# Five key and query projections as seven-block products, with three kinds of sums on GpSimd and PSUM banks 5+1+1+1

## The chip, the cores and the metric

The kernel runs on one core of a Trainium2 chip. The metric is the device time of one execution in microseconds (us). Engines are named as in the profile: PE is TensorE's matrix multiply and PEld its weight load, DVE is VectorE, ACT is ScalarE, POOL is GpSimd, and SP is SyncE, which here only issues transfers.

## The reference, cut to what matters

The reference is a two-layer encoder over 512 tokens of width 1024. Layer 0 has grouped-query and latent attention, layer 1 has neighbourhood attention (16 heads of 64), and each layer ends in a squared-ReLU MLP. The change touches layer 1's attention alone:

```python
def neighbourhood_attention(h, w_qkv, rpb, w_out):
    q, k, v = jnp.split(h @ w_qkv, 3, axis=-1)      # h is 512 x 1024, w_qkv 1024 x 3072
    ...                                              # 16 heads; 128-query blocks
    sc = jnp.einsum('bhqd,bhqkd->bhqk', qblk, kg) * scale + bias[None]
    p = jax.nn.softmax(sc, axis=-1)
    return jnp.einsum('bhqk,bhqkd->bhqd', p, vg)     # then @ w_out
```

## The kernel before

Every operand of a large product is split into a high and a low part in float32r, and a product is three passes on PE (high by high, high by low, low by high). Activations lie transposed, 1024 features as eight 128-row blocks (KD = 8), 512 tokens along the free axis.

**The seven-block product.** The MLPs of both layers already use class `Seven`. A pair of 128-row blocks of the contraction, a pair of output blocks and two halves of 256 tokens make a 2x2x2 block product, done with seven products of 128x128 by 256 in place of eight. It needs sums of the weight blocks (`seven_chunk`: three POOL operations on 128, 256 and 128 columns, then an ACT copy to the high part and a DVE subtraction to the low part, each on 896 columns), sums of the token blocks (`Seven.sums` and `Seven.split`), and a combination of the seven results (in `Seven.run`).

**Layer 1's attention.** After layer 0's MLP the kernel splits the eight token blocks (`split_g`, into `X`, read as `XP`), and runs two opening products by hand: `valuesC(0)`, the values of heads 0 to 3, and `projC(0)`, the keys and queries of the first pair of heads. While they run, `rows_r1` makes the RMS factor: POOL and DVE sum squares, PE adds them over partitions, DVE turns them into `r1` with three Newton steps (`rsqrt_steps`), and PE transposes `r1` so that `rb` is the factor broadcast over partitions. The order on each engine up to here comes from the tile scheduler.

Then `attend_C` runs the 16 heads one after another with an order fixed by hand (`fixed_order`): every engine does its instructions in the order in which the code emits them. For each head PE computes scores in two halves (`scores`, one `s` bank each), DVE adds the bias and takes the minimum, ACT takes the exponential (`weigh`), DVE the reciprocal, POOL multiplies (`norm`), and one head later PE transposes the result (`turn` with T1 and T2, one `t` bank each) and multiplies with the values (`finish`, one `o` bank). Between these steps `fill.run` places pieces of other products on PE: the seven remaining key and query projections `projC(1)` to `projC(7)`, the values `valuesC(1)` to `valuesC(3)`, and part of the output projection. How much is placed is set by `LEAD` before the first head and by `RATE_C` at six places in every head. Evacuations of these products are put off by `soon` and `soon_a` to the next `catch_up`.

`projC(t)` is a plain product: 8 blocks of the contraction, 2 output blocks (key and query), 3 passes, which is 48 matmuls of 128x512. Its weights come in two chunks of 1024 columns (`chunk`). Its key is evacuated by a DVE multiplication with `rb` and its query by two DVE operations with `rb`, then each is split and sent to the other partitions by transfers from POOL and SP.

PSUM has eight banks: three `mm`, two `s`, two `t` and one `o`, for the whole kernel.

## Time and profile before

| | |
|---|---|
| median of 3 runs | 1154.99 us (1154.98 to 1155.4) |
| span of the profiled execution | 1153.1 us |
| busy PE, DVE, ACT, POOL | 1143.5, 897.7, 668.3, 598.1 us |
| layer 1's 16 heads: first scores to last value product | 618.5 to 794.4 us |
| granted TensorE clock | 0.999 |

The profile has no time of its own for the profiled execution beside its span, which runs from the first to the last instruction; the median of the runs is 1.9 us longer. A duration in the timeline is that of one instruction; matmuls are pipelined, so that their pace is read from the starts of successive ones, not from their durations.

### The profile page before, as it was taken

Reading aid. Unit: us, or ns where it says so; the run is one execution under the profiler, and the core shown is the slowest. Engines: PE = TensorE matmul, PEld = TensorE weight load, DVE = VectorE, ACT = ScalarE, POOL = GpSimd, SP = SyncE. Lnnn points to the kernel's source line nnn. Section 1 sums busy time; section 2 is a strip of 40 time slices with the busy share of each in tenths; the row PEclk is TensorE's granted clock in tenths of the full one; section 3 lists DMA queues with packets and bytes.
Section 4 is the critical chain, followed back from the end, with each engine's and each line's share of the span. In section 5 each row is a group of like instructions: output and inputs, shape, how many; then the busy total and the mean of one; then the engine's idle time right before and its main releaser. Section 6 shows DMA issues by size and latency. Waiting matters only on the chain.

```text
span 1153.1 us, 20506 instructions
## 1 busy us (share of the span) xinstructions
PE 1143.5 (99%) x7348; PEld 1023.9 (89%) x7348; DVE 897.7 (78%) x1570; ACT 668.3 (58%) x1133; POOL 598.1 (52%) x722
## 2 busy tenths in 40 slices
PE   9999999999999999999999999999999999999997
PEld 8787888888899999899988998988889999989996
DVE  7887998988868787978775667668997777697874
ACT  6676786755346668534464556555553666773334
POOL 4356432327688992379432232231388889435740
PEclk9999999999999999999999999999999999999999
DMA  8322441223523335933585564443344233372432
GB/s 237 108 70 76 113 121 56 65 65 99 167 82 93 92 92 151 264 102 99 151 167 158 150 174 128 117 112 116 108 148 128 75 93 91 78 189 70 123 119 73
DMA packets 118325, 136.06 MB, mean 118 GB/s; under 512 B 9923, under 2 KB 99952, under 8 KB 118224
## 3 DMA queue, kind: packets, MB, share of 16 engines
q1 hardware_dynamic: 110736, 119.83, 35.2%
q0 software_dynamic: 7312, 14.83, 6.9%
q8 instruction: 58, 0.95, 0.3%
q14 instruction: 43, 0.35, 0.1%
q10 hardware_dynamic: 176, 0.10, 0.0%
HBM read 112.70 MB, written 6.29 MB: 103 GB/s over the span
## 4 chain that ended last, share of the span: by engine, by line
PE 93%; issue 3%; DVE 2%; ACT 1%; POOL 0%; POOLq 0%; DVEq 0%; ACTq 0%
PE mm L613 9%; PE mm L615 9%; PE mm L614 9%; PE mm L457 4%; PE mm L459 4%; PE mm L458 4%; PE t L457 3%; PE t L459 3%; PE t L458 3%; PE s L1138 3%; PE o L1126 3%; PE s L613 2%; PE s L615 2%; PE s L614 2%; PE s L457 2%
## 5 line engine op out<-in xcount | busy, mean ns | idle before, releaser
L370 DVE TENSOR_TENSOR wlo<-a,whi 128x896 fp32r<-128x896 f32 x106 | 131.4, 1243 | 57.9 <-ACT whi L369 57.5
L613 PE MATMUL mm<-a,whi 128*128 128x512 f32 x428 | 174.1, 407 | 0.1
L614 PE MATMUL mm<-a,whi 128*128 128x512 f32 x428 | 168.8, 394 | 0.0
L615 PE MATMUL mm<-a,wlo 128*128 128x512 f32 x428 | 168.5, 395 | 0.0
L369 ACT ACTIVATE whi<-a 128x896 fp32r<-128x896 f32 x106 | 100.6, 949 | 112.1 <-PE s L458 25.0
L223 DVE TENSOR_TENSOR wlo<-raw,whi 128x1024 fp32r<-128x1024 f32 (+4 forms) x93 | 105.9, 1144 | 27.3 <-ACT whi L233 26.9
L233 ACT ACTIVATE whi<-raw 128x1024 fp32r<-128x1024 f32 (+3 forms) x96 | 88.0, 918 | 59.5 <-PE s L614 24.8
L457 PE MATMUL mm<-a,whi 128*128 128x256 f32 x430 | 120.8, 281 | 0.0
L459 PE MATMUL mm<-a,wlo 128*128 128x256 f32 x430 | 120.6, 280 | 0.0
L458 PE MATMUL mm<-a,whi 128*128 128x256 f32 x430 | 120.5, 280 | 0.0
L369 ACT ACTIVATE whi<-raw 128x896 fp32r<-128x896 f32 x58 | 55.1, 953 | 83.3 <-PE s L458 24.4
L364 POOL TENSOR_TENSOR a<-a 128x256 f32<-128x256 f32 x104 | 95.7, 920 | 8.2
L365 POOL TENSOR_TENSOR a<-a 128x128 f32<-128x128 f32 x104 | 95.5, 919 | 8.2
L615 PEld LDWEIGHTS mm<-a,wlo 128*128 128x128 f32 x428 | 80.3, 188 | 18.3
L613 PEld LDWEIGHTS mm<-a,whi 128*128 128x128 f32 x428 | 80.6, 188 | 16.1 <-issue 0.6
L1146 POOL TENSOR_SCALAR p<-p,ti 128x512 f32<-128x512 f32 x64 | 47.0, 736 | 90.3 <-DVE ti L1145 67.0
L614 PEld LDWEIGHTS mm<-a,whi 128*128 128x128 f32 x428 | 80.7, 189 | 14.6
L370 DVE TENSOR_TENSOR wlo<-raw,whi 128x896 fp32r<-128x896 f32 x58 | 71.5, 1243 | 23.8 <-ACT whi L369 23.7
L1775 POOL TENSOR_SCALAR p<-p,ti 128x256 f32<-128x256 f32 x64 | 35.4, 564 | 104.7 <-DVE ti L1774 91.7
L457 PE MATMUL t<-a,whi 128*128 128x256 f32 x312 | 87.6, 281 | 0.0
L459 PE MATMUL t<-a,wlo 128*128 128x256 f32 x312 | 87.5, 280 | 0.0
L458 PE MATMUL t<-a,whi 128*128 128x256 f32 x312 | 87.5, 280 | 0.0
(449 smaller groups left out, 3602.4 us busy)
## 6 DMA issues: line engine op xcount, KB each, us to landing
a<-in_ffn_w_up_dram SPq DMA_DIRECT2D x102, 256.0 KB, 2.8
raw<-in_ffn_w_down_dram SPq DMA_DIRECT2D x34, 512.0 KB, 4.4
raw<-in_ffn_w_down_dram SPq DMA_DIRECT2D x56, 256.0 KB, 2.7
raw<-in_od_w_qkv_dram SPq DMA_DIRECT2D x64, 128.0 KB, 3.4
raw<-in_ffn_w_up_dram SPq DMA_DIRECT2D x12, 512.0 KB, 4.0
wlo<-in_ffn_w_down_dram POOLq DMA_DIRECT2D x12, 512.0 KB, 6.4
a<-a SPq DMA_DIRECT2D x17, 256.0 KB, 3.3
bx<-a SPq DMA_DIRECT2D x32, 128.0 KB, 5.2
```

What stands on the lines that cost most here:

```text
L223: z = lambda: (eng or DVE).tensor_tensor(to, src, f32(high), op=ALU.subtract)
L233: ACT.activation(hi[:, 0:m], raw[:, 0:m], AF.Copy)
L364: held(eng.tensor_tensor(r[:, 4:6], r[:, 2:3].to_broadcast([P, 2, P]), r[:, 0:7:6], op=ALU.add))
L365: held(eng.tensor_tensor(r[:, 7], r[:, 3], r[:, 5], op=ALU.subtract))
L369: ACT.activation(hi[:, 0:896], raw[:, 128:1024], AF.Copy)
L370: DVE.tensor_tensor(lo[:, 0:896], raw[:, 128:1024], f32(hi[:, 0:896]), op=ALU.subtract)
L457: PE.matmul(o, wh, x[:, 0], start=kp == 0 and n in (0, 1, 3, 5), stop=False, skip_group_check=True)
L458: PE.matmul(o, wh, x[:, 1], start=False, stop=False, skip_group_check=True)
L459: PE.matmul(o, wl, x[:, 0], start=False, stop=kp == self.np - 1, skip_group_check=True)
L613: PE.matmul(o, wh, xh, start=first, stop=False)
L614: PE.matmul(o, wh, xl, start=False, stop=False)
L615: PE.matmul(o, wl, xh, start=False, stop=last)
```

## The change

`projC(1)` to `projC(5)` become `projC7(1)` to `projC7(5)`. Four chunks of weights each (`seven_pair`, three POOL sums per chunk, always in one of four `raw` buffers) and 84 matmuls of 128x256 take the place of two chunks and 48 matmuls of 128x512. The key and query blocks of one pair of heads are the two output blocks of the seven-block product, so it needs four `mm` banks at once. The seven results are combined by four DVE operations, and the multiplications by `rb` move from DVE to POOL. The sums of the token blocks (`SevenC.sums`) are made once, while `projC(0)` runs, with three POOL operations for each of four pairs, and are kept in eight slots until `projC7(5)` has run. For `attend_C` alone the banks become five `mm`, one `s`, one `t` and one `o`. `RATE_C` goes from 1.33 to 1.26, and `valuesC` comes ahead of the projection of the same number.

```diff
+    def banks_for(name, **bufs):
+        psum[0].close()
+        psum[1:] = [psum[0].enter_context(tc.tile_pool(name=name, bufs=1, space=PSUM)), bufs]
+    banks_for("ps", mm=3, s=2, t=2, o=1)
...
+    def seven_pair(w, k0, t):
+        raw = wp.tile([P, 1024], F32, tag="raw", bufs=4, name=nm("raw"))
+        for k in range(2):
...
+        yield
+        POOL.tensor_tensor(r[:, 6], r[:, 0], r[:, 1], op=ALU.subtract)
+        POOL.tensor_tensor(r[:, 4:6], r[:, 2:3].to_broadcast([P, 2, P]), r[:, 0:7:6], op=ALU.add)
+        POOL.tensor_tensor(r[:, 7], r[:, 3], r[:, 5], op=ALU.subtract)
+        yield
...
+        ACT.activation(hi[:, 0:896], raw[:, 128:1024], AF.Copy)
+        yield hi, lo, [lambda: DVE.tensor_tensor(lo[:, 0:896], raw[:, 128:1024], f32(hi[:, 0:896]), op=ALU.subtract)]
...
+    class SevenC(Seven):
...
+        def sums(self, kp):
+            raw, t = Slot(F32), scratch()
+            for z in range(2):
+                ACT.activation(raw.t[:, S * z : S * z + S], hT[:, 2 * kp + z, :], AF.Copy, scale=gmix(1, 2 * kp + z))
+            yield
+            r, t_ = (x.rearrange("p (b n) -> p b n", n=256) for x in (raw.t, t))
+            POOL.tensor_tensor(t_, r[:, 0:1].to_broadcast([P, 2, 256]), r[:, 1:3], op=ALU.subtract)
+            POOL.tensor_tensor(r[:, 0], r[:, 2], t_[:, 0], op=ALU.subtract)
+            POOL.tensor_tensor(r[:, 1], r[:, 3], r[:, 0], op=ALU.subtract)
+            yield
+            for n, src in enumerate((t_, r[:, 0:2])):
...
+                ACT.activation(d[:, :, 0], src, AF.Copy)
+                DVE.tensor_tensor(d[:, :, 1], src, f32(d[:, :, 0]), op=ALU.subtract)
...
+    def projC7(t):
+        ids = [plan(w_qkv, 2 * kp, t, make=seven_pair) for kp in range(4)]
+        def ev(bk, half):
...
+            ACT.activation(Y[:, 0:256], half(bk[0], 0), AF.Copy)
+            def first():
+                DVE.tensor_tensor(two(X), two(Y)[:, 0:1].to_broadcast([P, 2, 256]), two(bk[1]), op=ALU.add)
+                DVE.tensor_tensor(two(Y), two(X)[:, 0:1].to_broadcast([P, 2, 256]), two(bk[2]), op=ALU.add)
+                soon(second)
+            def second():
+                DVE.tensor_tensor(X[:, 0:256], Y[:, 0:256], half(bk[2], 1), op=ALU.add)
+                DVE.tensor_tensor(Y, Y, bk[3], op=ALU.add)
+                POOL.tensor_tensor(nk[:, 0:256], Y[:, 256:512], rb[:, 0:256], op=ALU.mult)
+                POOL.tensor_tensor(nk[:, 256:512], X[:, 256:512], rb[:, 256:512], op=ALU.mult)
+                soon_a(lambda: split(nk, ka, down))
+                POOL.tensor_tensor(nq[:, 64:320], X[:, 0:256], rb[:, 0:256], op=ALU.mult)
+                POOL.tensor_tensor(nq[:, 320:512], Y[:, 0:192], rb[:, 256:448], op=ALU.mult)
+                POOL.tensor_tensor(nq[:, 0:64], Y[:, 192:256], rb[:, 448:512], op=ALU.mult)
+                soon_a(high)
...
+            bk = [mmb() for _ in range(4)]
...
+    parts = [xC.sums(kp) for kp in range(4)]
     for n, _ in enumerate(second):
         if n == 2:
             next(root)
+        if n % 2 == 1:
+            for kp in range(4):
+                if kp <= n // 2 < kp + 3:
+                    next(parts[kp])
...
     for t in range(1, 8):
-        fill.add(f"c{t}", projC(t))
         if t in (2, 4, 6):
             fill.add(f"c{t}", valuesC(t // 2, lambda: [mmb(), mmb()]))
+        fill.add(f"c{t}", projC7(t) if t < 6 else projC(t))
...
-    LEAD, RATE_C = 11.0, 1.33
+    LEAD, RATE_C = 11.0, 1.26
...
+    banks_for("psC", mm=5, s=1, t=1, o=1)
     fill.run(LEAD)
...
+    banks_for("psD", mm=3, s=2, t=2, o=1)
```

The change moves instructions on POOL and DVE at three places. The lines below carry the line numbers of the file they come from, so that `L262` before and `L268` after are the same statement.

**POOL while `projC(0)` runs, before.** The rows are POOL's queue from the accumulating transfers into `wlo`, the low parts of `projC(0)`'s weights (L262), to the transfers of the first keys (L1643) and queries (L1675, L1677).

```order
L262 DMA wlo_1237_6846<-in_od_w_qkv_dram 128x4x256
L262 DMA wlo_1243_6883<-in_od_w_qkv_dram 128x2x128 x4
L262 DMA wlo_1256_6946<-in_od_w_qkv_dram 128x2x128 x4
L1643 DMA a_1282_7160<-a_1282_7160 64x1024
L1643 DMA a_1283_7161<-a_1283_7161 64x1024
```

**The same place after.** L390 to L392 are `seven_pair`'s weight sums (in `raw`), L1664 to L1666 `SevenC.sums`' token sums (in `a` and `sc`).

```order
L268 DMA wlo_1256_6946<-in_od_w_qkv_dram 128x2x128 x4
L1664 TENSOR_TENSOR sc_1281_7134<-a_1280_7133 128x512
L390 TENSOR_TENSOR raw_1309_7263<-raw_1309_7263 128x128
L1665 TENSOR_TENSOR a_1280_7133<-a_1280_7133,sc_1281_7134 128x256
L391 TENSOR_TENSOR raw_1309_7263<-raw_1309_7263 128x256
L1666 TENSOR_TENSOR a_1280_7133<-a_1280_7133 128x256
L392 TENSOR_TENSOR raw_1309_7263<-raw_1309_7263 128x128
L1664 TENSOR_TENSOR sc_1284_7154<-a_1283_7153 128x512
L1665 TENSOR_TENSOR a_1283_7153<-a_1283_7153,sc_1284_7154 128x256
L1666 TENSOR_TENSOR a_1283_7153<-a_1283_7153 128x256
```

Behind the last accumulating transfer now stand four groups of token sums and two more groups of weight sums; two groups of weight sums stand between the transfers. The third group of token sums ends with the fifteenth operation behind that transfer, `a_1287`, and the fourth with the eighteenth, `a_1291`.

**DVE while it makes `r1`, before.** These rows are the end of the Newton steps and the copy of the result into `r1`.

```order
L187 TENSOR_TENSOR ti_1274_7079<-ti_1273_7077 128x4
L188 TENSOR_TENSOR ti_1274_7079<-ti_1274_7079,ti_1271_7072 128x4
L190 SCALAR_TENSOR_TENSOR ti_1275_7082<-ti_1274_7079,ti_1273_7077 128x4
L187 TENSOR_TENSOR ti_1276_7084<-ti_1275_7082 128x4
L188 TENSOR_TENSOR ti_1276_7084<-ti_1276_7084,ti_1271_7072 128x4
L190 SCALAR_TENSOR_TENSOR ti_1277_7087<-ti_1276_7084,ti_1275_7082 128x4
L1608 COPY r1_7061<-ti_1277_7087 128x4
```

**The same place after.** L1672 is the low part of the token sums, which DVE can only do when POOL has made the sum and ACT its high part.

```order
L193 TENSOR_TENSOR ti_1274_7079<-ti_1273_7077 128x4
L1672 TENSOR_TENSOR a_1296_7211<-sc_1288_7173,a_1296_7211 128x2x256
L194 TENSOR_TENSOR ti_1274_7079<-ti_1274_7079,ti_1271_7072 128x4
L1672 TENSOR_TENSOR a_1297_7214<-a_1287_7172,a_1297_7214 128x2x256
L196 SCALAR_TENSOR_TENSOR ti_1275_7082<-ti_1274_7079,ti_1273_7077 128x4
L193 TENSOR_TENSOR ti_1276_7084<-ti_1275_7082 128x4
L194 TENSOR_TENSOR ti_1276_7084<-ti_1276_7084,ti_1271_7072 128x4
L196 SCALAR_TENSOR_TENSOR ti_1277_7087<-ti_1276_7084,ti_1275_7082 128x4
L1635 COPY r1_7061<-ti_1277_7087 128x4
```

Two low parts of the third pair's sums (`a_1296` and `a_1297`, which read `sc_1288` and `a_1287`) now stand inside the chain that ends in `r1`.

**POOL in the first head, after.** L1781 to L1786 multiply the seven-block product's key and query by `rb`, L1797, L1810 and L1811 send them on, and L1902 is `norm` (before, L1775, with nothing but transfers between).

```order
L1785 TENSOR_TENSOR sc_1330_7401<-sc_1329_7400,rb_7145 128x192
L1786 TENSOR_TENSOR sc_1330_7401<-sc_1329_7400,rb_7145 128x64
L1902 TENSOR_SCALAR p_1343_7453<-p_1343_7453,ti_1344_7458 128x256
L1810 DMA a_1334_7406<-a_1334_7406 64x512
L1797 DMA a_1333_7405<-a_1332_7404 64x1024 x2
L1811 DMA a_1334_7406<-sc_1335_7407 64x512
L1902 TENSOR_SCALAR p_1343_7453<-p_1343_7453,ti_1345_7460 128x256
L390 TENSOR_TENSOR raw_1325_7368<-raw_1325_7368 128x128
L391 TENSOR_TENSOR raw_1325_7368<-raw_1325_7368 128x256
L392 TENSOR_TENSOR raw_1325_7368<-raw_1325_7368 128x128
L1902 TENSOR_SCALAR p_1347_7499<-p_1347_7499,ti_1348_7504 128x256
```

The product's multiplications and a group of weight sums now stand between the multiplications by which `norm` finishes a head's probabilities.

More of the change, by code (lines that the diff above doesn't have):

```diff
@@ L74, in free, with bank @@
             give(self.i)
-    def bank(tag, bufs):
-        return ps.tile([P, 512], F32, tag=tag, bufs=bufs, name=nm(tag))
+    def bank(tag):
+        return psum[1].tile([P, 512], F32, tag=tag, bufs=psum[2][tag], name=nm(tag))
     def mmb():
-        return bank("mm", 3)
+        return bank("mm")
     def sbk():
-        return bank("s", 2)
+        return bank("s")
     def stb():
-        return bank("t", 2)
+        return bank("t")
     def ob():
-        return bank("o", 1)
+        return bank("o")
     def scratch(dt=F32):
@@ L443, in plan, with products @@
                     for kp in range(self.np)]
-        def run(self, ids, evac):
-            bk = group(4)
-            half = lambda b, z: b[:, 256 * z : 256 * z + 256]
+        def products(self, ids, bk, half):
             dst = [(0, 0), (1, 1), (1, 0), (2, 1), (2, 0), (3, 1), (3, 0)]
@@ L460, in run @@
                     yield 0.355
+        def run(self, ids, evac):
+            bk = group(4)
+            half = lambda b, z: b[:, 256 * z : 256 * z + 256]
+            yield from self.products(ids, bk, half)
             w_ = Slot(F32)
@@ L1616, in rows_r1, with at, number @@
         yield
+    class SevenC(Seven):
+        def at(self, kp, b):
+            if b < 3:
+                return XP[2 * kp + (b + 1) // 2][:, :, 256 * ((b + 1) % 2) : 256 * ((b + 1) % 2) + 256]
+            return super().at(kp, b)
+        def number(self, kp, b):
+            return 4 * kp + b - 3
+        def sums(self, kp):
[9 more added lines that the diff above has]
+            for n, src in enumerate((t_, r[:, 0:2])):
+                s_ = self.slots[2 * kp + n] = Slot()
+                d = s_.t.rearrange("p (q z n) -> p q z n", q=2, z=2)
+                ACT.activation(d[:, :, 0], src, AF.Copy)
+                DVE.tensor_tensor(d[:, :, 1], src, f32(d[:, :, 0]), op=ALU.subtract)
+            raw.free()
+            yield
+    xC = SevenC(KD)
     PC = [{} for _ in range(8)]
```

48 lines of the change are left out of this document (45 added, 3 removed).

## Prediction

> **What bounds the kernel now.** I read the page's head first, then a table by stretches, then POOL's, DVE's and PE's timelines around the start of layer 1's attention.
>
> ```profile
> span 1153.1 us, 20506 instructions
> PE 1143.5 (99%) x7348; PEld 1023.9 (89%) x7348; DVE 897.7 (78%) x1570; ACT 668.3 (58%) x1133; POOL 598.1 (52%) x722
> ...
> PE 93%; issue 3%; DVE 2%; ACT 1%; POOL 0%; POOLq 0%; DVEq 0%; ACTq 0%
> ```
>
> PE is busy all the time and carries 93% of the chain that ends last. So a microsecond of PE work that goes is a microsecond won, and a microsecond for which PE is made to wait is lost; there is no slack that could swallow either. The stretches (us; busy PE, PEld, DVE, ACT, POOL; clock, DMA share, GB/s) say the same of the places that the change touches:
>
> ```profile
> 592.00:607.00 15.00, 15.00 (x87) 12.98 (x86) 7.97 (x23) 5.26 (x9) 3.74 (x4) 1.00 0.68 138
> 618.00:717.00 99.00, 99.00 (x629) 88.99 (x628) 64.89 (x186) 56.19 (x134) 29.33 (x56) 1.00 0.58 150
> ```
>
> The first is `projC(0)`, the second heads 0 to 8. POOL is the idlest engine there, but it is an in-order queue, and what counts is where its new work stands. These are the transfers that it issues during `projC(0)` (start, duration, idle before):
>
> ```profile
> 581.18 1.22 POOL L262 DMA_DIRECT2D wlo<-in_od_w_qkv_dram  x1 [0.74 <-ACT wlo L260]
> 586.50 3.65 POOL L262 DMA_DIRECT2D wlo<-in_od_w_qkv_dram  x3 [4.10 <-issue]
> 590.94 1.21 POOL L262 DMA_DIRECT2D wlo<-in_od_w_qkv_dram  x1 [0.79 <-ACT whi L265]
> ...
> 597.41 1.20 POOL L262 DMA_DIRECT2D wlo<-in_od_w_qkv_dram  x1 [0.56 <-issue]
> 607.44 0.58 POOL L1643 DMA_DIRECT2D a<-a  x1 [8.82 <-DVE a L1641]
> ```
>
> The accumulating transfers cost POOL 1.2 us each and are spread until 598.6; then it is free.
>
> **The matmuls that go.** The pace of matmuls is read from their starts:
>
> ```profile
> 578.25 0.40 PE L613 MATMUL mm<-a,whi 128*128 128x512 f32 x1
> ...
> 582.45 0.39 PE L613 MATMUL s<-a,whi 128*128 128x512 f32 x1
> ```
> ```profile
> 399.86 0.28 PE L457 MATMUL mm<-a,whi 128*128 128x256 f32 x1
> ...
> 402.33 0.28 PE L457 MATMUL mm<-a,whi 128*128 128x256 f32 x1
> ```
>
> Eighteen matmuls of 512 columns take 4.20 us, 0.2333 each; twenty-one of 256 in an existing seven-block product take 2.47, 0.1176 each. A projection goes from 48 x 0.2333 = 11.20 to 84 x 0.1176 = 9.88 us, five of them save 6.6 us. All of it is on the path. Between heads the wide ones go a little faster, eight in 1.85 us:
>
> ```profile
> 652.12 0.39 PE L613 MATMUL mm<-a,whi 128*128 128x512 f32 x1
> ...
> 653.97 0.39 PE L615 MATMUL mm<-a,wlo 128*128 128x512 f32 x1
> ```
>
> At that pace the saving is 6.1 us, which I keep as its lower bound.
>
> **The token sums and `r1`.** This is the largest term. Behind the last accumulating transfer POOL has fifteen operations until the third pair's sums are done: three groups of token sums and two of weight sums. The like of both stands in the MLP (duration as min/median/max):
>
> ```profile
> L397 POOL TENSOR_TENSOR a<-a x8: 1296/1743/2282, 265.9 to 837.3; 128x512 f32<-128x512 f32 x8
> ```
> ```profile
> L400 POOL TENSOR_TENSOR a<-a,a x8: 741/1066/1605, 267.8 to 839.1; 128x256 f32<-128x256 f32 x8
> ```
> ```profile
> L403 POOL TENSOR_TENSOR a<-a x8: 1069/1078/1604, 268.9 to 840.8; 128x256 f32<-128x256 f32 x8
> ```
> ```profile
> 265.94 1.73 POOL L397 TENSOR_TENSOR a<-a 128x512 f32<-128x512 f32 x1 [12.21 <-DVE a L1383]
> ...
> 281.92 0.96 POOL L363 TENSOR_TENSOR a<-a 128x128 f32<-128x128 f32 x1
> ...
> 317.08 0.46 POOL L363 TENSOR_TENSOR a<-a 128x128 f32<-128x128 f32 x1 [4.16 <-DMA a<-in_ffn_w_up_dram]
> ...
> 318.86 0.46 POOL L363 TENSOR_TENSOR a<-a 128x128 f32<-128x128 f32 x1
> ...
> 320.64 0.46 POOL L363 TENSOR_TENSOR a<-a 128x128 f32<-128x128 f32 x1
> ...
> 323.14 0.46 POOL L363 TENSOR_TENSOR a<-a 128x128 f32<-128x128 f32 x1
> ```
>
> Four groups of token sums took 16.0 us from 265.94 on, 4.0 each; from the minima and gaps of 0.08 a group could take 3.35. A group of weight sums took 1.78 (from 317.08) or 2.50 (from 320.64). So the fifteen cost between 3 x 3.35 + 2 x 1.78 = 13.6 and 3 x 4.0 + 2 x 2.5 = 17.0 us. I take 14.5, near the low end, since DVE, beside whose work POOL's operations grow, is busy for 8 of 15 us there and will itself be waiting. The two groups between the transfers find 0.79 us of idle time before a transfer here and 4.10 there; I cost them at nothing, at most at 2.5 us if the transfers aren't late enough to cover them. POOL is then done at 598.6 + 14.5 = 613.1 (612.2 to 618.1).
>
> DVE needs this in the middle of making `r1`. The chain there, the ACT and DVE operations in question (their group's mean) and the first instruction on PE that needs `r1`:
>
> ```profile
> 597.61 0.16 DVE L190 SCALAR_TENSOR_TENSOR ti<-ti,ti 128x4 f32<-128x4 f32 x1
> ...
> 598.39 0.21 DVE L1608 COPY r<-ti 128x4 f32<-128x4 f32 x1
> ```
> ```profile
> L971 DVE TENSOR_TENSOR a<-sc,a 128x512 fp32r<-128x512 f32 x14 | 9.9, 709 | 5.7 <-ACT a L974 5.7
> ...
> L974 ACT ACTIVATE a<-sc 128x512 fp32r<-128x512 f32 x14 | 8.8, 632 | 9.0 <-DVE sc L1090 4.6 <-DVE sc L1627 4.3
> ```
> ```profile
> 600.93 0.60 PE L642 MATMUL t<-cst,r 128*128 128x128 f32 x4
> ```
>
> After POOL come 0.63 us on ACT, 0.71 on DVE, 1.0 for the last five small steps and 0.1 for signals: `r1` is there at 615.5, and PE stands at its transposes from 600.93 on. That is a wait of **14.6 us** (13.7 to 19.6). The rest of `projC(0)` is queued behind it on PE, and ACT's values and `rb` wait for it too.
>
> **The change of banks.** Before, the first matmul of the next projection went to the free third `mm` bank. Now it waits for the query of `projC(0)` to leave its bank, which DVE does behind everything else it has to do after `r1`: two weight splits, four value evacuations, the key, two key splits and the last two token sums, then L1720 twice.
>
> ```profile
> 601.54 1.22 DVE L223 TENSOR_TENSOR wlo<-raw,whi 128x1024 fp32r<-128x1024 f32 x1 [0.43 <-ACT whi L233]
> 602.69 0.48 DVE L1737 SCALAR_TENSOR_TENSOR a<-s,r,a 128x256 fp32r<-128x256 f32 x1
> ...
> 605.05 0.69 DVE L1627 TENSOR_TENSOR sc<-mm,rb 128x512 f32<-128x512 f32 x1 [0.48 <-PE mm L615]
> ...
> 607.87 0.76 DVE L1660 SCALAR_TENSOR_TENSOR sc<-mm,rb 128x448 f32<-128x448 f32 x2
> ```
>
> By these rows that is 2 x 1.22 + 4 x 0.48 + 0.69 + 4 x 0.71 + 0.76 = 8.7 us, against 6.3 us of PE work left from 601.3 to 607.6: PE waits 2.4 us, with ACT in between some **3.0**. The bounds are 1.0 (the evacuation and its signals alone) and 3.5.
>
> **The heads.** To POOL's 29.3 us in 618 to 717 come fourteen groups of weight sums (25 to 35 us) and the five projections' multiplications by `rb`, 3.7 us each by the minima above and gaps of 0.08 (18 to 24): 73 to 88 of 99 us. POOL isn't the bound on average, but its queue is lumpy.
>
> ```profile
> L1775 POOL TENSOR_SCALAR p<-p,ti 128x256 f32<-128x256 f32 x64 | 35.4, 564 | 104.7 <-DVE ti L1774 91.7 <-PE o L1817 9.7 <-PE mm L1720 3.3
> ...
> L1653 POOL DMA_DIRECT2D a<-a x14 | 7.5, 539 | 15.8 <-DVE a L971 9.8 <-ACT p L1805 4.2 <-DVE ti L1786 1.8
> ```
>
> In the first head four multiplications (2.9), three of `norm` (1.7), four transfers (2.2) and a group of weight sums (1.8 to 2.5) stand in a row, 8.6 to 9.3 us, behind a DVE combination that ends some 3.7 us after the projection (three operations like L1627, one like L223 and a short one). PE wants the last of these `norm` after 87 matmuls of 256 columns and three small transposes, some 10.5 us: it waits about 2 us. Five projections end so, but the others have more before them: 0 to 13 us, I take one each, **5**. The single `s` and `t` banks cost nothing where `fill.run` stands between two uses; without that cover a use waits for L1798 and L1800, and that only ends the last head. ACT's and DVE's extra weight splits hide beside PE, as in the MLP.
>
> **The sum.** 1153.1 - 6.6 + 14.6 + 3.0 + 5.0 = 1169.1 us of span, and with the 1.9 us by which the median exceeds the profiled span **1171.0 us**.
>
> **A restart.** The kernel's only start from idle is its first: PE's first sixteen small matmuls against six like them a little later.
>
> ```profile
> 1.00 3.78 PE L157 MATMUL o<-ones 128*128 128x128 f32 x16 [1.00 <-POOL zeros L130]
> ...
> 5.83 1.06 PE L157 MATMUL o<-ones 128*128 128x128 f32 x6
> ```
>
> At 0.234 against 0.158 us each (less the last one's tail), the start lost 1.1 us, though the granted clock reads 1.00. If PE starts as slowly after the long wait, the time is 1172.1. The Trainium skill, "TensorE: Matmul & The Clock Gate", section "What's actually happening", says that the clock falls to half after an idle window of about 3.4 us and comes back after as long a busy one. By that rule an estimate is 1.7 us lost and a time of 1172.7; these rows agree that a start is slow, and the clock column does not show it.
>
> **The rivals.**
> - *The token sums are in time, and the change is faster.* POOL would have to end the third pair's sums by 598.5, where before it issued its last transfer at 597.41; each microsecond after that costs one. With the bank wait of 1 and nothing in the heads the time is 1155.0 - 6.6 + 1.0 = 1149.4, and the sign turns at a wait for `r1` of about 5 us. For it speaks only that those transfers wait on something (4.10 us of idle time), so that they could move; against it that fifteen operations stand behind the last. Chance 0.08.
> - *POOL binds the heads.* If every operation there grows to its slow form, 88 of 99 us are taken and each of the five evacuations costs 2.6: 13 instead of 5, and 17.0 instead of 14.5 at the start, 1181.5. For it: DVE gets more to do. Against: `norm`'s mean of 564 ns is near its short form. Chance 0.12.
> - *The slow restart* above: 1172.1, chance 0.25.
> - *Shorter waits of 3 to 8 us in all*, since the weight groups fill POOL's gaps and its transfers end 8 to 10 us sooner than the rows show: 1151 to 1157, chance 0.05.
>
> **The numbers.** My forecast has 0.50 and the time of 1171. Its own terms reach from 1155.0 - 6.6 + 13.7 + 1.0 = 1163 to 1155.0 - 6.1 + 19.6 + 3.5 + 13 = 1185. The low end of the range is set a little under this, at 1160, the high end at 1183, which leaves out the two fast cases and the tip of the slow one, 0.2 in all. A measurement of this kernel tells about 0.2%, 2.3 us, from no change. Slower by more than that: 0.50 + 0.25 + 0.12 + 0.01 = 0.88; within it 0.04; faster 0.08, the first rival.
>
> **What would show it.** PE idle for some 15 us just before its transposes of `r1`, with POOL busy without a break from about 599 to 613 and DVE waiting there for ACT's L1671 of the changed file; a wait of 1 to 3 us at the first 256-column matmul of `projC7(1)`; matmuls at 0.118 us from there on; waits of PE for POOL's `norm` in the heads after an evacuation. The forecast is wrong if PE's wait for `r1` is under 5 us, which means that POOL did its sums between or faster than in the MLP, or if the heads' waits exceed 13.

## The result and the profile after

The changed kernel takes 1200.87 us (median of 4 runs, 1200.05 to 1202.16) against 1155.08 us before (1154.98 to 1155.4): 1.0398 times as long, 95% interval 1.0383 to 1.0413, 45.8 us slower. The forecast had the sign right, but said 1171.0 with a range of 1160 to 1183.

The head of the page of after says where to look: PE is busy for 1151 us, 7 us more than before, and the span has grown by 45.2, so most of the loss is time in which PE stands.

```profile
span 1198.3 us, 21112 instructions
PE 1150.9 (96%) x7528; PEld 1037.1 (87%) x7528; DVE 928.8 (78%) x1593; ACT 688.5 (57%) x1164; POOL 669.4 (56%) x819
```

PE's timeline of after in layer 1's attention, only rows with long idle time (start, duration, instruction, in brackets the idle time before it and what ended it):

```profile
613.62 1.11 PE L669 MATMUL t<-cst,r 128*128 128x128 f32 x4 [12.64 <-DVE r L1635]
...
624.16 0.35 PE L478 MATMUL mm<-a,whi 128*128 128x256 f32 x1 [1.58 <-DVE sc L1720]
...
646.59 0.33 PE L1924 MATMUL t<-cst,p 128*128 128x128 f32 x1 [1.74 <-POOL p L1902]
...
672.17 0.39 PE L480 MATMUL mm<-a,wlo 128*128 128x256 f32 x1 [1.03 <-DVE wlo L397]
...
684.35 1.19 PE L1898 MATMUL s<-a,a 128*128 128x256 f32 x4 [5.54 <-DMA a<-sc]
...
731.72 0.39 PE L480 MATMUL mm<-a,wlo 128*128 128x256 f32 x1 [2.92 <-DVE wlo L397]
...
736.81 0.75 PE L1898 MATMUL s<-a,a 128*128 128x256 f32 x4 [3.30 <-DMA a<-sc]
...
783.25 0.72 PE L1898 MATMUL s<-a,a 128*128 128x256 f32 x4 [2.67 <-DMA a<-sc]
...
829.79 0.80 PE L642 MATMUL mm<-a,wlo 128*128 128x512 f32 x1 [1.75 <-DVE wlo L229]
...
835.10 0.50 PE L640 MATMUL mm<-a,whi 128*128 128x512 f32 x1 [1.74 <-DVE sc L1117]
```

The three rows of scores that wait for a transfer (`DMA a<-sc`) are the first scores of heads 4, 8 and 12, so of pairs 2, 4 and 6, the pairs whose projection the change puts behind the values. Pairs 1, 3 and 5 have the new evacuation too and wait for no transfer, while pair 6 still has the old projection. With five smaller ones (0.28 to 0.60 us) these rows come to 36.9 us: 12.6 for `r1`, 1.6 for the change of banks, 11.5 at scores that wait for a transfer of the query, 4.0 at matmuls whose low weights DVE has not split yet, 3.4 for `norm`, for the evacuation of transposes and for banks of an earlier projection, and 3.9 around the last head. In the kernel before no row of PE between 600 and 795 us has as much as 0.2 us of idle time.

The waits have a second price. The stretches behind them (first pair of numbers, then length, busy time of PE, PEld, DVE, ACT and POOL; the first of the last three numbers is the granted clock):

```profile
613.60:618.00 4.40, 4.38 (x13) 3.60 (x14) 3.52 (x6) 3.53 (x7) 0.00 (x0) 0.50 0.40 119
684.40:689.80 5.40, 5.40 (x26) 5.40 (x27) 3.25 (x9) 2.69 (x7) 4.74 (x9) 0.51 0.42 95
737.40:741.00 3.60, 3.60 (x20) 3.60 (x19) 2.79 (x7) 2.59 (x7) 0.00 (x0) 0.53 0.74 204
829.80:833.20 3.40, 3.40 (x12) 3.00 (x12) 2.97 (x5) 1.06 (x1) 0.00 (x0) 0.52 0.50 140
836.40:840.00 3.60, 3.60 (x10) 2.79 (x9) 0.04 (x1) 0.00 (x0) 0.00 (x0) 0.53 0.41 152
```

Here PE is busy without a break, but at half the clock. The starts of matmuls of 512 columns in the first stretch, four steps from the first row to the last:

```profile
615.39 0.63 PE L642 MATMUL mm<-a,wlo 128*128 128x512 f32 x1
...
617.09 0.63 PE L640 MATMUL mm<-a,whi 128*128 128x512 f32 x1
```

0.425 us each instead of 0.233. Of the 20.4 us in the five stretches 20.4 x (1 - 0.233 / 0.425) = 9.2 are lost. So 36.9 + 9.2 - 6.6 saved = 39.5 of the 45.2 us. Of the rest, 15 x 0.17 = 2.5 us hide in how idle time is read: a row's idle time counts from the modelled end of the matmul before, 0.40 us after its start, where the next could have started after 0.23. Some 3 us are not assigned: PE's idle time grew by 37.8 us (span less busy time, 9.6 before and 47.4 after), 0.9 more than the rows above, and the rest stands inside its busy time.

### The profile page after: what moved, and what is told of

It is laid out like the page before. It is cut to its first block, busy times and chain, and to the rows that moved or that the text cites. A ratio compares the mean times of both kernels' runs of the same rounds, so it can differ in the third digit from the quotient of the medians.

```text
span 1198.3 us, 21112 instructions
## 1 busy us (share of the span) xinstructions
PE 1150.9 (96%) x7528; PEld 1037.1 (87%) x7528; DVE 928.8 (78%) x1593; ACT 688.5 (57%) x1164; POOL 669.4 (56%) x819
## 5 line engine op out<-in xcount | busy, mean ns | idle before, releaser
L478 PE MATMUL mm<-a,whi 128*128 128x256 f32 x570 | 161.7, 284 | 2.8 <-DVE sc L1720 1.6
L480 PE MATMUL mm<-a,wlo 128*128 128x256 f32 x570 | 160.2, 281 | 4.1 <-DVE wlo L397 4.0
L479 PE MATMUL mm<-a,whi 128*128 128x256 f32 x570 | 159.8, 280 | 0.0
L640 PE MATMUL mm<-a,whi 128*128 128x512 f32 x348 | 142.8, 411 | 1.7 <-DVE sc L1117 1.7
L642 PE MATMUL mm<-a,wlo 128*128 128x512 f32 x348 | 138.5, 399 | 1.7 <-DVE wlo L229 1.7
L641 PE MATMUL mm<-a,whi 128*128 128x512 f32 x348 | 138.6, 398 | 0.0
L229 DVE TENSOR_TENSOR wlo<-raw,whi 128x1024 fp32r<-128x1024 f32 (+4 forms) x83 | 93.9, 1137 | 31.2 <-ACT whi L239 30.9
L239 ACT ACTIVATE whi<-raw 128x1024 fp32r<-128x1024 f32 (+3 forms) x86 | 77.4, 903 | 59.6 <-PE s L641 30.1
L480 PEld LDWEIGHTS mm<-a,wlo 128*128 128x128 f32 x570 | 107.5, 189 | 4.8 <-DVE wlo L397 4.7
L478 PEld LDWEIGHTS mm<-a,whi 128*128 128x128 f32 x570 | 107.6, 189 | 4.0 <-ACT whi L396 2.0
L479 PEld LDWEIGHTS mm<-a,whi 128*128 128x128 f32 x570 | 107.6, 189 | 0.1
L371 POOL TENSOR_TENSOR a<-a 128x128 f32<-128x128 f32 x104 | 100.9, 970 | 8.2
L375 ACT ACTIVATE whi<-raw 128x896 fp32r<-128x896 f32 x58 | 55.2, 954 | 83.7 <-POOL raw L371 24.9
L370 POOL TENSOR_TENSOR a<-a 128x256 f32<-128x256 f32 x104 | 92.5, 890 | 8.2
L369 POOL TENSOR_TENSOR a<-a 128x128 f32<-128x128 f32 x104 | 66.1, 636 | 34.5 <-DMA a<-in_ffn_w_up_dram 20.4
```

Of the source, the lines that this page charges most:

```text
L229: z = lambda: (eng or DVE).tensor_tensor(to, src, f32(high), op=ALU.subtract)
L239: ACT.activation(hi[:, 0:m], raw[:, 0:m], AF.Copy)
L370: held(eng.tensor_tensor(r[:, 4:6], r[:, 2:3].to_broadcast([P, 2, P]), r[:, 0:7:6], op=ALU.add))
L371: held(eng.tensor_tensor(r[:, 7], r[:, 3], r[:, 5], op=ALU.subtract))
L375: ACT.activation(hi[:, 0:896], raw[:, 128:1024], AF.Copy)
L478: PE.matmul(o, wh, x[:, 0], start=kp == 0 and n in (0, 1, 3, 5), stop=False, skip_group_check=True)
```

## The experiments

Three parts of the change were put into the kernel before one at a time, and parts of the changed kernel were undone or mended one at a time and together, so that the rival causes of the waits could be set against each other. All ratios are to the kernel before.

**The banks alone.** The order, the projections and the rate of the kernel before, but:

```diff
+    banks_for("psC", mm=5, s=1, t=1, o=1)
     fill.run(LEAD)
...
+    banks_for("psD", mm=3, s=2, t=2, o=1)
```

> The kernel before, with nothing changed but the banks of layer 1's attention (5+1+1+1 instead of 3+2+2+1). Theory A (the heads' loss in the changed kernel comes from late transfers of the query and key, not from the banks): only the waits at the two changes of banks and around the last head stay, 1.6 + 0.8 + 3.5 us by the trace of the changed kernel, some of them with a slow clock behind: 2 to 7 us slower, 1157 to 1162. Rival B (the single s bank and the single t bank tie scores, transposes and their evacuations together all along the heads): 15 us or more slower, over 1170.

1163.99 us, ratio 1.0074 (1.0059 to 1.0089): 8.7 us slower, a little above A and far from B. PE's long waits there, of which there is but one more, 0.97 us at the first matmul behind the first change of banks (608.45, just behind DVE's last read of an old bank, L1720, and a weight split on ACT):

```profile
792.67 0.66 PE L1924 MATMUL t<-cst,p 128*128 128x128 f32 x4 [1.44 <-DVE a L1927]
795.30 1.14 PE L1944 MATMUL o<-a,a 128*128 128x256 f32 x8 [1.97 <-DVE sc L1117]
797.84 0.80 PE L640 MATMUL mm<-a,whi 128*128 128x512 f32 x1 [1.40 <-DVE sc L1117]
```

All three stand around the last head: the second group of transposes waits for its only `t` bank, the value products for the only `o` bank, and the first matmul after the change of banks for DVE's last read of that same bank (L1117). In the sixteen heads ahead of them the single banks cost nothing on PE.

**The end of the heads mended**, in the kernel with the banks alone:

```diff
-        turn(prev, *T2, [])
+        turn(prev, *T2, [], mmb)
         catch_up()
         fill.until("out")
+        finish_off()
+        banks_for("psD", mm=3, s=2, t=2, o=1)
         finish(prev)
```

> The kernel before with the banks 5+1+1+1, and at the end of the heads the last group of transposes in a bank of mm and the change of banks ahead of the last head's value products. Theory J (what the banks alone cost, 8.7 us, is the three waits of 1.4, 2.0 and 1.4 us around the last head and the slow clock behind them): 5 to 7 us faster than with the banks alone, 1157 to 1159. Rival B (the single banks cost in every head): 1162 or more.

1158.88 us, ratio 1.0032 (1.002 to 1.0044). J holds: 5.1 of the 8.7 us come back. What is left is 0.97 us at the start and one wait of 2.80 us at the new change of banks with a slow stretch behind.

**The token sums alone**, made and used by nothing, in the kernel before (banks, order, rate and projections as before):

```diff
+    parts = [xC.sums(kp) for kp in range(4)]
     for n, _ in enumerate(second):
         if n == 2:
             next(root)
+        if n % 2 == 1:
+            for kp in range(4):
+                if kp <= n // 2 < kp + 3:
+                    next(parts[kp])
```

> The kernel before, with the token sums made as in the changed kernel and not used by any projection; banks, order and rate as before. Theory A (POOL's and ACT's steps of the sums stand in front of r1 on DVE): the wait of 12.6 us at the transposes of r1 shrinks a little, since two groups of weight sums are no longer in POOL's queue, to 8 to 12 us, and 1.9 us of slow clock follow: 10 to 14 us slower, 1165 to 1169. Rival C (the weight sums of the first seven-block projection are what delays the token sums): under 5 us slower, below 1160.

1168.09 us, ratio 1.0109 (1.0094 to 1.0124), 12.8 us slower: A. The wait at the transposes of `r1` is 10.79 us, with slow clock to 617.2. So the token sums are the largest loss of the three parts that were put into the kernel before alone (banks 8.7, sums 12.8, order 2.3, below).

**The token sums on DVE**, in the changed kernel:

```diff
-            POOL.tensor_tensor(t_, r[:, 0:1].to_broadcast([P, 2, 256]), r[:, 1:3], op=ALU.subtract)
-            POOL.tensor_tensor(r[:, 0], r[:, 2], t_[:, 0], op=ALU.subtract)
-            POOL.tensor_tensor(r[:, 1], r[:, 3], r[:, 0], op=ALU.subtract)
+            DVE.tensor_tensor(t_, r[:, 0:1].to_broadcast([P, 2, 256]), r[:, 1:3], op=ALU.subtract)
+            DVE.tensor_tensor(r[:, 0], r[:, 2], t_[:, 0], op=ALU.subtract)
+            DVE.tensor_tensor(r[:, 1], r[:, 3], r[:, 0], op=ALU.subtract)
```

> The changed kernel with the three token-sum operations of each head pair on DVE instead of POOL. Theory A (the wait for r1 is the handing to and fro between POOL, ACT and DVE, and DVE's small operations are slow while POOL adds: 0.7 to 1.25 us instead of 0.16, one split 3.98): twelve sums are 6.1 us of DVE work that mostly lies before 600, the wait for r1 falls from 12.6 to 2 to 5 us, and the slow clock behind it may go: 8 to 12 us faster than the changed kernel, 1189 to 1193. Rival D (DVE's amount of work is what counts): no gain or up to 4 us slower, 1200 to 1205.

1190.95 us, ratio 1.0306 (1.0289 to 1.0323): 9.9 us faster than the changed kernel, A. In its trace PE waits for `r1` only this long:

```profile
604.93 0.65 PE L669 MATMUL t<-cst,r 128*128 128x128 f32 x4 [2.79 <-DVE r L1635]
```

DVE gets some 6 us more work, and its result comes 8.7 us sooner. Why is seen in the timeline of DVE and POOL in the changed kernel:

```profile
598.56 3.98 DVE L1672 TENSOR_TENSOR a<-sc,a 128x512 fp32r<-128x512 f32 x1 [5.57 <-ACT a L1671]
...
606.21 1.26 POOL L1664 TENSOR_TENSOR sc<-a 128x512 f32<-128x512 f32 x1
606.31 1.19 DVE L187 TENSOR_SCALAR ti<-ti 128x4 int32<-128x4 int32 x1
...
608.64 0.73 POOL L1666 TENSOR_TENSOR a<-a 128x256 f32<-128x256 f32 x1
...
609.33 1.80 POOL L1664 TENSOR_TENSOR sc<-a 128x512 f32<-128x512 f32 x1
609.91 1.25 DVE L194 TENSOR_TENSOR ti<-ti,ti 128x4 f32<-128x4 f32 x1
611.08 0.68 DVE L1672 TENSOR_TENSOR a<-a,a 128x512 fp32r<-128x512 f32 x1
...
613.40 0.17 DVE L1635 COPY r<-ti 128x4 f32<-128x4 f32 x1
```

The steps on four columns that make `r1` (L187, L194) take up to 1.25 us here while POOL adds beside them. Between 604.7 and 613.6 eight of them took 0.37 to 1.25 us, and each of the eight ends 0.01 to 0.03 us after the end of one of POOL's sums: L187 at 607.50 and POOL's L1664 at 607.47, L194 at 611.16 and POOL's next L1664 at 611.13. A split of token sums, 0.68 us at 611.08, took 3.98 at 598.56; no single POOL operation explains that one. With the sums on DVE, and POOL through with its weight sums, the same step takes

```profile
602.76 0.15 DVE L194 TENSOR_TENSOR ti<-ti,ti 128x4 f32<-128x4 f32 x1
```

**PE kept busy during the wait for `r1`**, in the changed kernel, with work that the transposes then overwrite:

```diff
         bk = stb()
+        for _ in range(52):
+            PE.matmul(bk, XP[0][:, 0, 0:128], XP[0][:, 0, :], start=True, stop=True, skip_group_check=True)
         bcast_cols(lambda i: r1[:, i : i + 1].to_broadcast([P, P]), P, bk)
```

> The changed kernel with 52 useless matmuls of 512 columns on PE in front of the transposes of r1, about the 12 us that PE stands idle there; they write the bank that the transposes then fill, so nothing in the result changes. Theory H (the clock is at half because PE stood idle): the stretch of clock 0.5 after the wait goes and r1 comes as before, 1.8 us faster than the changed kernel, about 1199. Rival I (the clock fell for another reason, or a busy PE costs as much elsewhere): no difference.

1201.2 us, ratio 1.04 (1.0377 to 1.0422): no difference that can be seen, though the runs spread from 1198.98 to 1204.45 and the 1.8 us of H are not excluded by them. H holds for the clock; for the time its own trace speaks against it. The stretch after the wait now reads

```profile
613.00:618.00 5.00, 3.41 (x18) 2.57 (x17) 4.53 (x11) 2.40 (x6) 1.42 (x2) 1.00 0.14 34
```

with a clock of 1.00, so it is PE's idleness that halves the clock. But `r1` came 1.35 us later in this run (PE's transposes at 614.97; 612.5 to 614.6 in the other runs with the same start), and the first seven-block projection started at 624.00 instead of 624.16, since it waits for DVE's evacuation of the query and not for PE. A faster PE just ahead of a wait for another engine only waits longer (2.14 us there instead of 1.58).

**The projection ahead of the values**, as before the change:

```diff
     for t in range(1, 8):
+        fill.add(f"c{t}", projC7(t) if t < 6 else projC(t))
         if t in (2, 4, 6):
             fill.add(f"c{t}", valuesC(t // 2, lambda: [mmb(), mmb()]))
-        fill.add(f"c{t}", projC7(t) if t < 6 else projC(t))
```

> The changed kernel with each projection ahead of the values in the queue of filling work, as before the change. Theory A (the values-first order leaves a projection's evacuation, eleven operations and six transfers in a chain of some 20 us, too little time before the heads that need it): the waits for transfers of 5.5, 3.3 and 2.7 us go with the slow clock behind them, 2.7 and 1.7 us: 10 to 16 us faster than the changed kernel, 1185 to 1191. Rival E (the transfers are late because SP's and POOL's queues are blocked, whatever the order): the waits move to other heads, 0 to 4 us faster, 1197 to 1201.

1195.73 us, ratio 1.0348 (1.0333 to 1.0364), 5.1 us faster: between the two. The three waits for transfers are gone whole, as A says, but others have come, as E says:

```profile
659.56 0.52 PE L1924 MATMUL t<-cst,p 128*128 128x128 f32 x3 [1.87 <-DVE a L1927]
663.27 0.48 PE L1924 MATMUL t<-cst,p 128*128 128x128 f32 x1 [3.19 <-POOL p L1902]
...
694.18 0.73 PE L1898 MATMUL s<-a,a 128*128 128x256 f32 x4 [3.42 <-DVE ti L1913]
...
715.22 0.33 PE L1924 MATMUL t<-cst,p 128*128 128x128 f32 x1 [2.55 <-POOL p L1902]
```

The chain behind the first two, of the same kernel, ACT, DVE and POOL:

```profile
656.16 0.64 ACT L1001 ACTIVATE a<-sc 128x512 fp32r<-128x512 f32 x1 [5.01 <-POOL sc L1782]
...
658.24 0.52 ACT L1925 ACTIVATE a<-t 128x448 fp32r<-128x448 f32 x1
...
658.79 0.62 DVE L1927 TENSOR_TENSOR a<-t,a 128x448 fp32r<-128x448 f32 x1 [4.44 <-ACT a L1925]
...
660.56 1.10 POOL L1797 DMA_DIRECT2D a<-a  x2 [2.89 <-ACT p L1932]
```

ACT stands 5.0 us for POOL's second multiplication by `rb`, with the evacuation of the transposes (L1925) queued behind; DVE stands 4.4 us for that, with its reductions behind; POOL then stands 2.9 us, with four transfers and `norm` behind. One evacuation stops three in-order queues in turn.

**The multiplications on DVE**, on top of the order:

```diff
-                POOL.tensor_tensor(nk[:, 0:256], Y[:, 256:512], rb[:, 0:256], op=ALU.mult)
+                DVE.tensor_tensor(nk[:, 0:256], Y[:, 256:512], rb[:, 0:256], op=ALU.mult)
...
```

and so for all five.

> The kernel with the projection ahead of the values, and the five multiplications by rb of each projection on DVE instead of POOL. Theory A (those five on POOL are the link: ACT stands 5.0 and 3.7 us idle for them with the evacuation of transposes queued behind, DVE stands 4.4 us for ACT, then PE for norm, the t bank and the s bank): the waits of 1.9, 3.2, 3.4, 2.6 and 1.1 us in the heads mostly go, with 4.4 us of slow clock: 9 to 15 us faster than with the order alone, 1181 to 1187. Rival F (the weight sums on POOL are what norm waits for): under 4 us faster, 1192 or more. Rival G (DVE then binds): no gain.

1186.94 us, ratio 1.0269 (1.025 to 1.0287): 8.8 us faster than with the order alone, at the edge of A; F and G fall. The same edit in the changed kernel, without the order:

> The changed kernel with the five multiplications by rb of each projection on DVE instead of POOL, and the values still ahead of the projection. It completes the square: neither 1200.9, order alone 1195.7, both 1186.9. Theory A (the multiplications on POOL are the link, and each evacuation gets some 2.5 us shorter): the three waits for transfers, 5.5, 3.3 and 2.7 us, each lose 1 to 3 us, and the waits for weight splits behind the idle DVE (1.0 and 2.9) go: 6 to 12 us faster than the changed kernel, 1189 to 1195. Rival L (with the values first the transfers are late in any case, so the multiplications matter only with the order): under 4 us faster, 1197 or more.

1196.31 us, ratio 1.036 (1.0343 to 1.0378): 4.6 us faster than the changed kernel, between A and L. The waits for transfers only fell to 4.97, 1.86 and 2.42 us. The square is 1200.9 with neither, 1195.7 with the order, 1196.3 with the multiplications, 1186.9 with both: 13.9 us for both, 9.7 for the two added. The 4.2 us of excess are hardly more than the four intervals allow; they would fit two links in one chain, of which each stands behind the other.

**The order alone in the kernel before:**

```diff
     for t in range(1, 8):
-        fill.add(f"c{t}", projC(t))
         if t in (2, 4, 6):
             fill.add(f"c{t}", valuesC(t // 2, lambda: [mmb(), mmb()]))
+        fill.add(f"c{t}", projC(t))
```

> The kernel before with nothing changed but the order: the values ahead of the projection in the queue of filling work. It takes some 11 us of lead from the projections of pairs 2, 4 and 6. Theory A (the order alone makes transfers late, as the third wait of the changed kernel, at an old projection, suggests: 2.7 us and 1.6 of slow clock): 3 to 8 us slower, 1158 to 1163. Rival N (the old evacuation is short enough for the shorter lead, so that only both together cost): under 2 us slower.

1157.3 us, ratio 1.0019 (1.0009 to 1.0029), 2.3 us slower, between the two and nearer to N. Two waits of scores for the query's transfer appear, 0.55 and 0.77 us, at the first scores of heads 8 and 12, and one of 0.65 us for `norm`. So the shorter lead is all but enough for the queues as they were; in the changed kernel the transfers miss the scores by 2.7 to 5.5 us.

**No serial transfers**, in the changed kernel. The last transfers of key and query (L1793, L1815) overwrite what earlier ones (L1797, L1810) still read, so they start only when those have landed. SP's waits for that between 670 and 790 us (in total, times, longest) and the issues ahead of the wait at 684.35, in the changed kernel:

```profile
SPq L1793 <- DMA a<-a: 10.8, 2, 8.3
```
```profile
674.35 0.53 POOL L1810 DMA_DIRECT2D a<-a  x1
...
678.28 0.71 SPq L1793 DMA_DIRECT2D a<-a  x1
679.10 0.52 SPq L1815 DMA_DIRECT2D a<-sc  x1
```

The last lands at 684.2. The kernel before has the same pairs of transfers: SP waits for them there 13.1 us in four times between 600 and 795 us (its L1649), and no score waits. The edit lays out key and query as `projC(0)` does:

```diff
-                ACT.activation(q[:, 0, :], nq, AF.Copy, scale=0.125)
+                ACT.activation(lo[64:128, :], nq[64:128, :], AF.Copy, scale=0.125)
+                ACT.activation(q[0:64, 0, :], nq[0:64, :], AF.Copy, scale=0.125)
...
-                SP.dma_start(f32(q[64:128, 0, :]), f32(lo[0:64, :]))
+                POOL.dma_start(f32(q[64:128, 0, :]), f32(lo[0:64, :]))
```

and so for the low halves and the key.

> The changed kernel with the key and query of pairs 1 to 6 laid out as pair 0's: ACT and DVE write each half where it belongs, and four transfers that wait for no other transfer replace six of which two wait until others have landed; ACT and DVE get two operations more each per projection. Theory A (the two rounds of transfers, some 4.2 and 5.1 us one after the other, are what makes the scores late): the waits of 5.5, 3.3 and 2.7 us fall to 0 to 2 each, with their slow clock: 8 to 14 us faster than the changed kernel, 1187 to 1193. Rival M (the queues of ACT, DVE and POOL are what is late, and they get more to do): under 4 us faster, 1197 or more.

1201.14 us, ratio 1.0402 (1.0387 to 1.0418): no gain, M's time. But its trace has no score that waits for a transfer; the same time stands elsewhere:

```profile
691.65 1.22 PE L1903 MATMUL s<-a,a 128*128 128x256 f32 x4 [4.94 <-DVE ti L1918]
...
736.23 0.58 PE L480 MATMUL mm<-a,wlo 128*128 128x256 f32 x1 [4.66 <-DVE wlo L397]
```

**The repairs together**: token sums and multiplications on DVE, the order, the end of the heads.

> The changed kernel with the token sums and the multiplications by rb on DVE, the projection ahead of the values, and at the end of the heads the last group of transposes in a bank of mm and the change of banks ahead of the last head's value products. If the four causes add up: 9.9 for the sums, 5.1 for the order, 9 to 15 for the multiplications and 5 for the end: 1166 to 1172, still over the kernel before. Rival G (DVE, which takes 16 us more, binds): 1175 to 1185.

1175.99 us, ratio 1.018 (1.0165 to 1.0195): 24.9 us of the 45.8 are back, 4 us short of the measured gains added up (9.9 + 13.9 + 5.1 = 28.9). The time is at the low end of G. PE still waits 17.7 us: 3.3 for `r1`, 2.8 for the banks, 2.8 at the end, 8.9 in the heads, most of it for `norm`. The largest of those, POOL's timeline of this kernel and what PE does then:

```profile
648.65 1.11 POOL L1797 DMA_DIRECT2D a<-a  x2 [2.97 <-ACT p L1932]
649.76 0.53 POOL L1810 DMA_DIRECT2D a<-a  x1
...
650.28 0.53 POOL L1811 DMA_DIRECT2D a<-sc  x1
...
650.84 0.93 POOL L1902 TENSOR_SCALAR p<-p,ti 128x256 f32<-128x256 f32 x2
651.38 0.48 PE L1924 MATMUL t<-cst,p 128*128 128x128 f32 x1 [3.21 <-POOL p L1902]
```

Three more tries start from it. The layout without serial transfers:

> The four repairs and the layout without serial transfers. In the four repairs no score waits for a transfer any more. Theory A: so nothing is gained there; the waits for norm lose a little, since POOL's transfers stand elsewhere, and DVE and ACT get more: 1173 to 1179. Rival O (POOL's queue, held up by transfers that wait for DVE, was the rest of the loss): 5 us faster or more, under 1171.

1179.97 us, ratio 1.0216 (1.0201 to 1.0231): 4 us slower, a little beyond A, and O falls. PE waits 19.5 us instead of 17.7, with one stretch of slow clock more; that the extra operations on ACT and DVE are the reason was not tested. `norm` on DVE instead of POOL:

```diff
-            POOL.tensor_scalar(p, p, tt[:, 2:3], 1.0, op0=ALU.mult, op1=ALU.mult)
+            DVE.tensor_scalar(p, p, tt[:, 2:3], 1.0, op0=ALU.mult, op1=ALU.mult)
```

> The kernel with all four repairs (token sums and multiplications by rb on DVE, projection ahead of the values, the end of the heads), and norm's multiplication on DVE instead of POOL too. Theory A (norm stands in POOL's queue behind transfers that wait for DVE): PE's four waits for norm, 3.2, 1.3, 1.4 and 0.4 us, and 1.5 us of slow clock go: 4 to 8 us faster than with the four repairs, 1168 to 1172. Rival G (DVE, 76 of 99 us busy there, gets 13 us more and everything behind it comes later): 1176 to 1183.

1172.54 us, ratio 1.0154 (1.0138 to 1.017), 3.4 us faster, just short of A; G falls. And the first pair by the old projection in the old banks, with the token sums beside it and behind `r1`:

```diff
+        fill.add(f"c{t}", projC7(t) if 1 < t < 6 else projC(t))
...
+    while any(n == "c1" for n, _ in fill.q):
+        fill.step()
...
+                    next(parts[kp])
...
     banks_for("psC", mm=5, s=1, t=1, o=1)
```

> The four repairs, but the first pair after the opening keeps the old projection in the old banks, and the token sums are made beside it, behind r1; four projections instead of five are seven-block products, 1.3 us less saved. Theory A (what is left at the start is the wait for r1, 3.3 us, the wait for the banks, 2.8 us, and 3.1 us of slow clock): the first goes whole with its slow clock, the second shrinks to 1 to 2 us: 3 to 7 us faster than with the four repairs, 1169 to 1173. Rival K (the sums on DVE then delay the weight splits of that projection, a new wait): 1175 or more.

1172.07 us, ratio 1.0148 (1.0131 to 1.0164), 3.9 us faster, A's number; but where the waits for `r1` and for the banks go, one of 5.81 us comes ahead of the first scores (625.47). The profile names no releaser for it; DVE's last read of an old bank (L1720), which stands behind token sums in DVE's queue, ends at 625.25, so it may be the change of banks, made late by the sums: akin to K, but not K's weight splits. Both:

> Both together: late token sums with four seven-block projections, and norm on DVE. If they add: 1161 to 1168, still above the kernel before (1155), since 1.7 to 5 us at the end of the heads and their slow clock stay and only 5.3 us are saved. Rival G (DVE binds): 1172 or more.

1172.87 us, ratio 1.016 (1.0143 to 1.0177): they don't add; the time is G's, the cause is not shown. The last three times lie within each other's intervals. No version tried comes near the kernel before; the best is 17 us above it.

## Why the prediction was right and wrong

- **The matmuls that go: right.** In after, 21 of 256 columns take 2.49 us between the two rows below, 0.1186 each against 0.1176. The saving itself, 6.6 us, was not measured alone.

```profile
624.58 0.28 PE L478 MATMUL mm<-a,whi 128*128 128x256 f32 x1
...
627.07 0.28 PE L478 MATMUL mm<-a,whi 128*128 128x256 f32 x1
```

- **The wait for `r1`: right in mechanism, 12.6 instead of 14.6 us**, under its own low bound of 13.7. POOL was through with the third pair's sums not at 613.1 but at 609.4. All fifteen operations stood behind the last transfer, as I had it, but they took 13.3 us, not 14.5, and began 2.5 us earlier, since the last four transfers ran without the gaps between them that they have in the kernel before:

```profile
591.59 4.94 POOL L268 DMA_DIRECT2D wlo<-in_od_w_qkv_dram  x4
596.09 1.76 POOL L1664 TENSOR_TENSOR sc<-a 128x512 f32<-128x512 f32 x1
```

  The chain behind them took 4.2 us, not 2.4, as DVE's small steps stretch while POOL adds. I had POOL's operations grow beside DVE's, not DVE's beside POOL's. The sums alone cost 12.8 us. In the runs with the same start the wait was between 11.3 and 13.3 us.
- **The change of banks: right at the start**, 1.6 us for 3.0 (1.0 to 3.5). **Wrong at the end:** that the single banks "cost nothing where `fill.run` stands between two uses" held in the heads, and "that only ends the last head" was the place that I priced at nothing. There, and at the change back, the banks alone cost 4.8 us of waits and a slow clock, 5.1 us of which the mended end gave back.
- **The heads: this is the step that failed.** I priced 5 us (0 to 13) for `norm` behind POOL's lumps. The heads waited 18.8 us, only 1.7 of them at `norm`. POOL (the last of the five busy times) had about the load that I gave it, 73 to 88 us in heads 0 to 8, which now run from 634.6 to 749.0; it stood idle for a third of that time, so its amount of work was not the limit:

```profile
634.60:749.00 114.40, 97.81 (x774) 95.02 (x773) 75.23 (x190) 61.19 (x138) 74.46 (x121) 0.96 0.50 129
```

  I had followed one consumer of the evacuation. The keys and queries have another, the scores of the heads that they are for, and I did not ask how long the new evacuation takes to reach them, nor what the swap of values and projection takes from its lead, though the diff has it. Those waits were 11.5 us, all at the pairs that the swap sets back, one of them at an old projection. But neither the order nor the transfers are the cause by themselves: the order alone costs 2.3 us in the kernel before, and without serial transfers the waits moved to DVE with nothing gained. What the runs show in place of my 5 us: order and multiplications together gave back 13.9 us, the trace with the order alone has the evacuation stop ACT, DVE and POOL one after the other, and which wait PE meets changes with the order.
- **The restart: right in kind, one instead of five.** The rival had 1.1 us, or 1.7, after one wait. After 12.6 us of idle time the first stretch lost 4.4 x (1 - 0.233 / 0.425) = 2.0. I gave it to the wait for `r1` alone; the waits of 5.5 and 3.3 us and two of 1.7 did the same, and the five stretches lost 9.2 us. That is what they hold, not what undoing them would give back: with PE kept busy ahead of `r1` the 2.0 us went and the time stayed.
- **The rivals.** Token sums in time: no. POOL binds the heads, 1181.5: its mechanism, every operation in its slow form, did not come (74.5 us of work, not 88), though moving POOL's multiplications helped. My limits for a wrong forecast named heads' waits over 13 us, and that is what happened.

The span was forecast at 1169.1 and is 1198.3. The 29.2 us between are 13.8 more in the heads, 3.9 at the last head, 9.2 of slow clock, 3.4 less at the start, and 5.7 that no wait or clock above accounts for.

What stays open: the four repairs leave 21 us above the kernel before, of which 17.7 are waits on PE, and three more tries took off 4 us at most. Whether another order of the evacuation's operations in the three queues would bring the seven-block form to a gain was not tried. Nor was the lower `RATE_C` tried by itself, which sets how much of the filling work is placed in each head.

## What to carry to other kernels

Where PE is busy all the time, a product with fewer multiplications pays only if its sums and its longer evacuation fit into the queues that the path already uses; count every hand-over between in-order engines, and what stands behind each, not busy time. For a step that is moved or made longer, follow each of its results to its first use and compare the lead before and after. And price a wait on PE by more than its length: here one of 1.7 us or more could take another 1.6 us of slow clock, which counts only where PE is not about to wait for something else anyway.

## What the hardware showed unexpectedly

- **The clock halves after short waits, for whole windows.** Summed from the clock in slices of 0.2 us, the slow stretches between 590 and 880 us lasted 3.4, 6.8, 10.2 or 13.7 us in all the traces (idle time included), multiples of 3.41. No lone wait under 1.7 us was followed by one, every wait over 3.5 us was, and between it went both ways: 1.98 us with a slow stretch (at 679.09, `norm` on DVE), 3.42 us without (at 694.18, the order alone). That would fit windows which are slow once PE stands idle in about half of one, though no run set the wait apart to test it. The Trainium skill, "TensorE: Matmul & The Clock Gate", section "What's actually happening", gives a free-running window of 3.4 us and half the clock, 1.2 GHz, after an idle one; the lengths agree, and so do the 0.425 us per 512 columns (0.427 by 1.2 GHz, an estimate), but here a window need not be idle from end to end.
- **DVE's smallest operations pay for POOL's sums.** A Newton step on 128x4 took 0.15 to 0.16 us beside a quiet POOL and up to 1.25 us beside its token sums, ending when one of those sums ended. The Trainium skill, "SBUF — State Buffer", section "SBUF: two separate sides", says that GpSimd and DVE, the latter in operations with two inputs in SBUF or in a two-port mode, share a pair of ports which the one that starts first holds for its whole instruction while the other stops; the ends of the eight stretched steps agree. Moving 12 sums to DVE made DVE's result come 8.7 us sooner.
